# Quarter sums of weights: 29 of 128 additions moved from VectorE into accumulating transfers, in an encoder block on one core

## The chip, the cores and the metric

The kernel runs on one core of a Trainium2 chip. The metric is the device time of one execution in microseconds (us). The engines that matter here are TensorE (PE in the profile, PEld for its weight loads), VectorE (DVE), ScalarE (ACT), GpSimd (POOL), which also issues the DMAs that add while they write, and SyncE (SP), which issues the plain loads.

## The reference

One layer of an encoder on 512 tokens of width 1024, all in float32:

```
h    = RMSNorm(x);  proj = h @ W_in                      # 1024 x 11264
y_a  = (B * dwconv3(C * x_c)) @ W_a                      # 1024 x 1024
y_r  = (GroupNorm(Ret_fwd + Ret_bwd) * silu(G)) @ W_r    # 2048 x 1024, 4 heads
x    = x + (sigmoid(gA) * y_a + sigmoid(gR) * y_r) @ W_o # 1024 x 1024
h2   = RMSNorm(x)
x    = x + (silu(h2 @ W_gate) * (h2 @ W_up)) @ W_down    # 1024 x 2816, 2816 x 1024
y    = RMSNorm(x)
```

The result has to keep float32 accuracy.

## The kernel before, in words

**Split products.** Every float32 operand is split in two numbers that TensorE takes at full rate: `split` (L200) lets ACT round the source into `hi` (a CAST at L203), and VectorE subtracts, `lo = source - hi` (L204). A product is then three matmuls: hi hi, hi lo and lo hi.

**Seven products instead of eight.** Most weight matrices are used as quads: two by two quarters b11, b12, b21, b22. Strassen's scheme in Winograd's form multiplies seven combinations instead of eight quarters. On the weight side the seven forms are b11, b21, b22 and four sums (`FORMS`, L55):

```
t1 = b11 + b12      t2 = b11 + b12 + b22      t4 = b11 + b12 + b22 + b21
t3 = b12 + b22
```

The sums are made in place, in the tiles into which the quarters were loaded: t1, t2 and t4 one after the other in b11's tile, t3 in b12's. `prefetch_form` (L290) does this with an addition on VectorE (L301), and then splits the tile into `whi` and `wlo`. The tiles come from three pools: ten `raw` buffers for quarters, five `whi` and five `wlo` for split units of 128 x 1024.

**The quads.** There are six of the input projection (kind `w`; the first of them, at column `C_V`, is the first head's), three of the convolution columns (`x`), W_a (`a`), W_o (`o`), eleven of gate and up (`f`, 0 to 10, called pairs below, since b11 and b21 belong to gate, b12 and b22 to up), and three of W_down (`d`, after pairs 2, 6 and 10; the number in the quad is its first pair). Kinds `w`, `a`, `o` and `d` take two units for each form (u = 0 and 2), the others one. For three quads, `SUMMED` (pairs 0 and 1, and W_o), the four sums are made in DRAM long before by copies and accumulating DMAs (`sum_step`, L265), and are loaded as they are. For the other quads the 128 additions at L301 are made: 48 for `w`, 12 for `x`, 8 for `a`, 36 for `f` and 24 for `d`.

**The order.** `plan()` (L71) lists all units in the order in which TensorE uses them. `take()` (L321) hands out the next unit and calls `prefetch()` (L306) until two further units (`AHEAD`) are split; `prefetch` first calls `load_raws` (L281), which issues the loads of quarters that the plan needs within four more places (`LEAD`). So a unit's load, addition, cast and subtraction stand in the source some two products ahead of its own matmuls. What each engine executes in which order is fixed when the program is built, from estimates of when each instruction can run; it can differ from the order in the source.

**A pair** (`pair`, L1173) takes, from pair 5 on, the forms t1, t2, b21, t3, b11 of the next pair, t4, b22; from pair 2 to 4 the forms t1, t2, t3, one b11 or b21 of a later pair, t4, b22. Pairs 2 to 4 have used their own b11 and b21 earlier (`FIRST_PRODUCTS`, `beside`). Each form is one product of 24 matmuls (L383). The products t2, t3 and t4 add onto one bank of PSUM; `snap` (L432, a copy by ACT at L434) reads it out between them: u2 after t2, u3 after t3. `gated` (L1125) makes the activations for `down`.

**Down** (`strassen`, L437, with `prod_tm`, L409) uses the seven forms with 12 matmuls (L427) for a full unit. The first `down` stores its parts in DRAM (`put_first`, L1210); `add_first` (L1213) then adds them to `ydr` by eight accumulating DMAs of 256 KB on POOL, placed behind a small GpSimd operation (`mark`, L1247) that reads a tile which `gated` made in pair 3. The second `down` adds to `ydr` at L1208. The last one is written out at L1302 and reads `ydr` by accumulating DMAs into SBUF (`snap_y`, L1264).

Of the kernel before, what the change touches and what calls it, by code (L numbers as in the profile page):

```python
# [15 lines left out]
ALU = mybir.AluOpType  # L16
# [13 lines left out]
C_XC, C_GB, C_GC, C_Q, C_K, C_V, C_G, C_GA, C_GR = (  # L30
    0, 1024, 2048, 3072, 4096, 5120, 7168, 9216, 10240)
# [113 lines left out]


SUMMED = (("f", 0), ("f", 1), ("o",))


def parts(quad):  # L150
    return (0, 2) if quad == ("o",) else (0,)


def loads():
# [3 lines left out]
    for i, x in enumerate(PLAN):  # L158
        if x[0] == "q":
            _, quad, name, u, nk = x  # L160
            need = name if quad in SUMMED else NEEDS.get(name)
            if need:
                out.append((i, quad, need, u, nk * WIDTH[quad[0]]))
    return out + [(len(PLAN), quad, "b12", u, QH) for quad in SUMMED for u in parts(quad)]

# [6 lines left out]
def block_kernel(ctx: ExitStack, tc: tile.TileContext, xw0, xw, xT, xtok, wpack, wquad, cols, decs, rot, g_ffn, g_final, out):  # L172
    nc = tc.nc
# [14 lines left out]
    def bigtile(dt=F32, n=4):  # L188
        return big.tile([P, n, 512], dt, tag="big", name="big", padded_shape=[P, 4, 512])
# [10 lines left out]
    def split(src, hi, lo, scale=None, round=None):  # L200

        if scale is None:
            first = (round or nc.scalar.copy)(hi, src)  # L203
            low_of[0] = nc.vector.tensor_tensor(out=lo, in0=src, in1=hi.bitcast(F32), op=ALU.subtract)  # L204
        else:
            first = nc.scalar.activation(hi, src, AF.Copy, scale=scale)
            nc.vector.scalar_tensor_tensor(
                out=lo, in0=src, scalar=scale, in1=hi.bitcast(F32),
                op0=ALU.mult, op1=ALU.subtract)
        return first  # L210
# [10 lines left out]
    pos = [0]  # L221
# [5 lines left out]
    def unit():  # L227
        hi = wpool.tile([P, QH], F32R, tag="whi", name="whi")
        lo = wpool.tile([P, QH], F32R, tag="wlo", name="wlo")
        return hi, lo  # L230

    def prefetch_block(loads, splits):
        i = block[0]
        block[0] += 1
        st = [rawtile(), rawtile()]
        units = []
        for c in range(2):
            if loads:
                loads(c)
            nc.sync.dma_start(st[c], wpack[i][:, c * QH:(c + 1) * QH])  # L240
        for c in range(2):
            hi, lo = unit()
            units.append((hi, lo))
            split(st[c], hi, lo)
            if splits:
                splits(c)
        return units

    raws = {}

    wsum = {(quad, f, u): dram.tile([P, QH], F32, name="_".join(map(str, (f, u, *quad))))
            for quad in SUMMED for u in parts(quad) for f in ("t1", "t2", "t3", "t4")}

    def quarter(quad, name, u):
        return wquad[next(i for i, x in enumerate(QUARTERS) if x[1:4] == (quad, name, u))]

    def sums_of(quads):
        return [(quad, f, g, u, add) for group in (
            (("t1", "b11", 0), ("t3", "b22", 0)), (("t1", "b12", 1), ("t3", "b12", 1)),
            (("t2", "t1", 0),), (("t2", "b22", 1),), (("t4", "t2", 0),), (("t4", "b21", 1),))  # L260
            for quad in quads for f, g, add in group for u in parts(quad)]

    steps = {"quads": sums_of(SUMMED[:2]), "heads": sums_of(SUMMED[2:])}

# [16 lines left out]
    def load_raws(upto):  # L281
        while loaded[0] < len(LOADS) and LOADS[loaded[0]][0] <= upto:
            _, quad, name, u, n = LOADS[loaded[0]]
            t = rawtile()
            src = wsum[quad, name, u] if name[0] == "t" else quarter(quad, name, u)
            nc.sync.dma_start(t[:, 0:n], src[:, 0:n])
            raws[quad, name, u] = t
            loaded[0] += 1

    def prefetch_form(quad, f, u, nk):  # L290


        n = nk * WIDTH[quad[0]]
        if quad in SUMMED:
            here, more = f, None
        else:
            here = {"t1": "b11", "t2": "b11", "t4": "b11", "t3": "b12"}.get(f, f)
            more = {"t1": "b12", "t2": "b22", "t4": "b21", "t3": "b22"}.get(f)
        t = raws[quad, here, u][:, 0:n]
        if more:  # L300
            nc.vector.tensor_tensor(out=t, in0=t, in1=raws[quad, more, u][:, 0:n], op=ALU.add)  # L301
        hi, lo = unit()
        split(t, hi[:, 0:n], lo[:, 0:n])
        return [(hi, lo)]

    def prefetch(first=False, loads=None, splits=None):  # L306
        i = pos[0]
        if i >= len(PLAN):
            return False
        pos[0] += 1  # L310
        x = PLAN[i]
        if not first:
            load_raws(i + LEAD)
        if x[0] == "c":
            units = prefetch_block(loads, splits)
        else:
            units = prefetch_form(*x[1:])
        ready.append((x, units))
        return True

    def take():  # L321
        if not ready:
            prefetch()
        x, units = ready.pop(0)
        while sum(len(u) for _, u in ready) < AHEAD and prefetch():
            pass
        return x, units
# [203 lines left out]
    def split_two(k):  # L531
        split_x(k)
        split_x(k + 1)
    prefetch(True, lambda c: load_x(4 + 2 * c), lambda c: split_two(4 + 2 * c))
    rcs = misctile(D, "rcs").rearrange("p (i n) -> p i n", i=2)
    nc.sync.dma_start(rcs, rot)
# [101 lines left out]
    for h in range(EARLY):  # L638
# [27 lines left out]
        t = bigtile()  # L666
# [281 lines left out]
    for h in range(HEADS):  # L948
# [5 lines left out]
        t = sg  # L954
# [469 lines left out]
```

## Time and profile before

| What | us |
|---|---|
| median of 3 runs (1023.52 to 1023.67) | 1023.57 |
| span of the profiled execution | 1021.7 |
| TensorE busy in that span | 1013.2 |
| VectorE busy | 902.5 |
| ScalarE busy | 548.4 |
| GpSimd busy | 151.7 |

The profiled execution is one of its own; its span runs from the first to the last instruction of the program. The other times in the text are read from its trace.

How to read the lines: a row of the groups gives line, engine, operation, the tile written and the tiles read, shapes and count; behind the bar the busy time of the group in us, the mean of one in ns, and the idle time of the engine just before them, with what ended it. A row of the chain or of a timeline starts with the time from the span's start and the duration. A row of the windows gives the stretch, its length, and for PE, PEld, DVE, ACT and POOL the busy us with the number of instructions, then the granted share of TensorE's clock, the busy share of the DMA engines and GB/s. A row of the DMA view ends with KB for each and the median time from issue to landing. TensorE's clock was granted in full over the span (mean 0.999).

### The profile page before, as it was taken

Reading aid. Unit: us, or ns where it says so; the run is one execution under the profiler, and the core shown is the slowest. Engines: PE = TensorE matmul, PEld = TensorE weight load, DVE = VectorE, ACT = ScalarE, POOL = GpSimd, SP = SyncE. Lnnn points to the kernel's source line nnn. Section 1 sums busy time; section 2 is a strip of 40 time slices with the busy share of each in tenths; the row PEclk is TensorE's granted clock in tenths of the full one; section 3 lists DMA queues with packets and bytes.
Section 4 is the critical chain, followed back from the end, with each engine's and each line's share of the span. In section 5 each row is a group of like instructions: output and inputs, shape, how many; then the busy total and the mean of one; then the engine's idle time right before and its main releaser. Section 6 shows DMA issues by size and latency. Waiting matters only on the chain.

```text
span 1021.7 us, 14821 instructions
## 1 busy us (share of the span) xinstructions
PE 1013.2 (99%) x5586; PEld 883.2 (86%) x5586; DVE 902.5 (88%) x1161; ACT 548.4 (54%) x744; POOL 151.7 (15%) x238
## 2 busy tenths in 40 slices
PE   9999999999999999999999999999999999999997
PEld 7888888888888998888888888889998999899986
DVE  7878998979798888797989997999898999889996
ACT  7547665553655455343543325586654565556554
POOL 0030221222122003202122100020001410110011
PEclk9999999999999999999999999999999999999999
DMA  9525587695767657839597855484316562663523
GB/s 354 188 81 185 173 296 212 214 310 162 249 196 238 250 203 268 333 130 349 124 331 294 272 200 169 157 264 132 107 42 242 172 154 83 198 153 104 165 69 98
DMA packets 53992, 202.34 MB, mean 198 GB/s; under 512 B 7392, under 2 KB 7520, under 8 KB 49312
## 3 DMA queue, kind: packets, MB, share of 16 engines
q1 hardware_dynamic: 37600, 137.39, 39.0%
q0 software_dynamic: 16032, 63.71, 21.3%
q8 instruction: 44, 0.72, 0.3%
q10 hardware_dynamic: 288, 0.29, 0.1%
q14 instruction: 28, 0.23, 0.1%
HBM read 162.82 MB, written 57.41 MB: 216 GB/s over the span
## 4 chain that ended last, share of the span: by engine, by line
PE 98%; DVE 1%; ACT 0%; issue 0%; POOL 0%; POOLq 0%; ACTq 0%
PE bank L427 39%; PE bank L383 27%; PE bank L342 10%; PE bank L343 10%; PE bank L344 10%; PE bank L477 0%; PE bank L1053 0%; PE bank L998 0%; PE bank L662 0%; DVE raw L301 0%; DVE big L1296 0%; ACT whi L203 0%; DVE wlo L204 0%; POOL fin L1286 0%; POOL ac L1035 0%
## 5 line engine op out<-in xcount | busy, mean ns | idle before, releaser
L203 ACT CAST whi<-raw 128x1024 fp32r<-128x1024 f32 (+2 forms) x299 | 302.8, 1028 | 265.0 <-PE bank L427 67.1
L204 DVE TENSOR_TENSOR wlo<-raw,whi 128x1024 fp32r<-128x1024 f32 (+2 forms) x300 | 352.7, 1192 | 68.0 <-ACT whi L203 67.7
L383 PE MATMUL bank<-xform,whi 128*128 128x256 f32 x1424 | 258.2, 284 | 0.3 <-ACT whi L203 0.3
L383 PEld LDWEIGHTS bank<-xform,whi 128*128 128x128 f32 x1424 | 222.3, 192 | 2.0 <-ACT t L434 0.8
L383 PE MATMUL bank<-xform,wlo 128*128 128x256 f32 x712 | 200.7, 283 | 0.0
L427 PE MATMUL bank<-whi,big 128*128 128x512 f32 x596 | 187.0, 389 | 0.0
L427 PE MATMUL bank<-whi,xform 128*128 128x512 f32 x496 | 157.1, 390 | 0.0
L301 DVE TENSOR_TENSOR raw<-raw 128x1024 f32<-128x1024 f32 (+1 forms) x128 | 152.0, 1203 | 4.2 <-DMA raw<-wquad 3.3
L383 PEld LDWEIGHTS bank<-xform,wlo 128*128 128x128 f32 x712 | 136.4, 192 | 0.0
L427 PEld LDWEIGHTS bank<-whi,big 128*128 128x128 f32 x596 | 111.9, 188 | 23.8 <-ACT t L434 0.4
L427 PE MATMUL bank<-wlo,big 128*128 128x512 f32 x298 | 115.7, 389 | 0.0
L427 PEld LDWEIGHTS bank<-whi,xform 128*128 128x128 f32 x496 | 93.0, 188 | 19.7 <-DVE xform L204 0.6
L427 PE MATMUL bank<-wlo,xform 128*128 128x512 f32 x248 | 96.5, 389 | 0.0
L434 ACT COPY t<-bank 128x512 f32<-128x512 f32 x105 | 61.0, 587 | 56.3 <-PE bank L383 30.1
L342 PE MATMUL bank<-big,whi 128*128 128x512 f32 x220 | 85.7, 390 | 0.0
L344 PE MATMUL bank<-big,wlo 128*128 128x512 f32 x220 | 85.6, 389 | 0.0
L343 PE MATMUL bank<-big,whi 128*128 128x512 f32 x220 | 85.6, 389 | 0.0
L427 PEld LDWEIGHTS bank<-wlo,big 128*128 128x128 f32 x298 | 56.0, 188 | 11.4
L427 PEld LDWEIGHTS bank<-wlo,xform 128*128 128x128 f32 x248 | 46.6, 188 | 9.6
L342 PE MATMUL bank<-whi,big 128*128 128x512 f32 x128 | 49.8, 389 | 0.0
L343 PE MATMUL bank<-wlo,big 128*128 128x512 f32 x128 | 49.8, 389 | 0.0
L344 PE MATMUL bank<-whi,big 128*128 128x512 f32 x128 | 49.8, 389 | 0.0
(203 smaller groups left out, 1385.8 us busy)
## 6 DMA issues: line engine op xcount, KB each, us to landing
raw<-wquad SPq DMA_DIRECT2D x140, 512.0 KB, 4.7
raw<-wpack SPq DMA_DIRECT2D x42, 512.0 KB, 6.3
t_f<-wquad POOLq DMA_DIRECT2D x12, 512.0 KB, 8.0
z<-t POOLq DMA_DIRECT2D x24, 256.0 KB, 4.5
t_o<-wquad POOLq DMA_DIRECT2D x12, 512.0 KB, 6.7
zform<-z POOLq DMA_DIRECT2D x6, 1024.0 KB, 7.8
v<-t POOLq DMA_DIRECT2D x16, 256.0 KB, 5.7
sg<-t POOLq DMA_DIRECT2D x16, 256.0 KB, 4.8
```

Source lines behind the costliest of these rows:

```text
L203: first = (round or nc.scalar.copy)(hi, src)
L204: low_of[0] = nc.vector.tensor_tensor(out=lo, in0=src, in1=hi.bitcast(F32), op=ALU.subtract)
L301: nc.vector.tensor_tensor(out=t, in0=t, in1=raws[quad, more, u][:, 0:n], op=ALU.add)
L342: nc.tensor.matmul(ps, lh, rh, start=first, stop=False)
L343: nc.tensor.matmul(ps, lh, rl, start=False, stop=False)
L344: nc.tensor.matmul(ps, ll, rh, start=False, stop=last)
L383: nc.tensor.matmul(o, l[:, c], r[:, k], start=start and s == 0 and k == 0 and i == 0, stop=stop and k == 3 and i == 2, skip_group_check=True)
L427: nc.tensor.matmul(pss[tt], l, r[:, c], start=start and k == 0 and i == 0, stop=stop and k == n - 1 and i == 2, skip_group_check=True)
L434: nc.scalar.copy(t, ps)
```

## The change

A predicate `joined(quad, name)` is new. It holds for t3 and t4 of W_a, of the three `down` quads and of the first head's quad, and for t4 alone of pairs 2 to 10. For these units L301 is left out. The addition is made by a DMA on POOL's queue instead, which reads the second quarter from DRAM and adds it to the tile in SBUF: b22 onto b12's tile once t1 has read it, b21 onto b11's tile once t2 was split. The DMA is put on a list when t1 or t2 is prefetched, and issued in the source at the end of the same call of `prefetch` for pairs, one call later for the others. The quarters b21 and b22 are loaded for their own products as before.

```
+def joined(quad, name):
+    kind = quad[0]
+    if quad in SUMMED or name not in ("t3", "t4"):
+        return False
+    return kind in "ad" or kind == "f" and name == "t4" or kind == "w" and quad[1] == C_V

 in prefetch_form:
-        if more:
+        if more and not joined(quad, f):
             nc.vector.tensor_tensor(out=t, in0=t, in1=raws[quad, more, u][:, 0:n], op=ALU.add)
         hi, lo = unit()
         split(t, hi[:, 0:n], lo[:, 0:n])
+        for g, after, src, add in (("t3", "t1", "b12", "b22"), ("t4", "t2", "b11", "b21")):
+            if f == after and joined(quad, g):
+                late.append((pos[0] + (quad[0] != "f"), raws[quad, src, u], quarter(quad, add, u), n))
         return [(hi, lo)]

+    late = []
+    def join_late():
+        while late and late[0][0] <= pos[0]:
+            _, t, src, n = late.pop(0)
+            nc.gpsimd.dma_start(out=t[:, 0:n], in_=src[:, 0:n], accum_op=ALU.add)

 at the end of prefetch:
         ready.append((x, units))
+        join_late()
         return True
```

## The prediction

> **What bounds the kernel now.** I read the page from the top: busy times, then the chain that ended last, then TensorE's own waits, and then the few microseconds in which TensorE was not working.
>
> ```profile
> span 1021.7 us, 14821 instructions
> PE 1013.2 (99%) x5586; PEld 883.2 (86%) x5586; DVE 902.5 (88%) x1161; ACT 548.4 (54%) x744; POOL 151.7 (15%) x238
> PE 98%; DVE 1%; ACT 0%; issue 0%; POOL 0%; POOLq 0%; ACTq 0%
> L301 DVE TENSOR_TENSOR raw<-raw 128x1024 f32<-128x1024 f32 (+1 forms) x128 | 152.0, 1203 | 4.2 <-DMA raw<-wquad 3.3
> ```
>
> TensorE is busy 1013.2 of 1021.7 us and carries 98% of the chain. VectorE is at 88%, but it matters only where TensorE waits for it. The additions at L301, which the change thins out, take 152.0 us of an engine that is not the limit. So the question is how much of TensorE's 8.5 idle us lies behind them. The view of waits, kept to TensorE, and the last of the 25 us windows answer it:
>
> ```profile
> PE bank L477 <- DVE t L474: 1.4, 1, 1.4
> PE bank L1053 <- DVE t L1039: 0.5, 1, 0.5
> PE bank L383 <- ACT whi L203: 0.3, 1, 0.3
> 1000.00:1025.00 25.00, 15.61 (x69) 12.58 (x68) 14.21 (x24) 9.65 (x22) 4.11 (x8) 0.93 0.22 85
> ```
>
> The first wait, 1.4 us, is the start of the program. The second, 0.5 us, is the norm ahead of the FFN. In the last window TensorE works 15.6 us, so it ends near 1015.6, and 6.1 us of final evictions and stores follow. The sum 1.4 + 0.5 + 0.3 + 6.1 is 8.3 of the 8.5 us. Only the 0.3 us has a weight split behind it, and the chain of waits shows what stood there:
>
> ```profile
> 756.88 24.86 PE bank L427 x108
> 781.74 0.84 DVE raw L301
> 782.58 0.28 issue
> 782.85 1.22 DVE wlo L204
> 784.07 2.28 DVE raw L301 x2
> 786.43 1.06 ACT whi L203
> 787.53 73.91 PE bank L383 x612
> ```
>
> This is the passage from the first `down` to pair 3. An addition on VectorE, a subtraction, two more additions, then ACT's cast, and TensorE goes on. It is the one place in the span where L301 ends a wait of TensorE.
>
> **What is removed.** `joined` holds for t3 and t4 of W_a (2 units each: 4), of the first head (4), of the three `down` quads (12), and for t4 of pairs 2 to 10 (9): 29 of the 128 additions. At the mean of 1.203 us that is 34.9 us of VectorE. Almost all of it lies beside matmuls that do not wait, and is worth nothing; the most it can give back is the 0.3 us above. Four of the 29 lie in that first `down`, two of them at full width, and for pairs 2 to 4 the b21 tile is no longer held until t4's addition, which frees a raw buffer earlier. Both bring pair 3's splits forward by more than 0.3 us, so I take the wait as gone. What is late next there is nothing that TensorE sees: it then runs straight on. **Gain 0.3 us.**
>
> **What is added.** 29 accumulating DMAs on the POOL queue, nearly all of 512 KB, about 14.7 MB. POOL must issue them in its order, and the cast and the subtraction of t3 or t4 now wait for a landing. The trace has no DMA that adds 512 KB into SBUF. Its neighbours are the plain loads, the adds of 256 KB into SBUF, and the adds of 512 KB from DRAM to DRAM at L272 (the last row, from the view of that line):
>
> ```profile
> raw<-wquad SPq DMA_DIRECT2D x140, 512.0 KB, 4.7
> big<-ydr POOLq DMA_DIRECT2D x4, 256.0 KB, 4.5
> L1268 POOL DMA_DIRECT2D big<-ydr x4 | 3.5, 954 | 90.2 <-ACT big L1267 90.2
> ```
>
> ```profile
> DMA to landing us min/median/max: 5.4/8.0/13.1
> ```
>
> Twice the bytes of `big<-ydr` cannot be quicker than it, so 4.5 us is the lower end. The upper end is 13.1, the longest at L272. I take 6.0, between the add into SBUF and the median of 8.0, and nearer the quickest at L272: the destination is SBUF, and in the pairs few of POOL's DMAs run at once. POOL's own work, 29 times 0.95 or 28 us, goes onto an engine at 15%. While a new DMA waits there for t1's or t2's reads, what is queued behind it waits too: the first head's stores, the load of `ga` beside W_a, and the stores of `down`. POOL's timeline shows them:
>
> ```profile
> 95.53 1.14 POOL L633 DMA_DIRECT2D v<-t  x2 [20.48 <-DVE t L448]
> 595.46 0.53 POOL L973 DMA_DIRECT2D big<-ga  x1 [13.07 <-DVE big L939]
> 773.64 1.20 POOL L1211 DMA_DIRECT2D first_part<-t  x2 [85.15 <-DVE t L448]
> ```
>
> POOL stood idle 20, 13 and 85 us before them, for VectorE's results; the reads that a new DMA waits for belong to units that come before those results. I cost this queueing at 0; held by one transfer's issue it would be 1 us of a store that TensorE does not wait for. SP's loads stay the same in number.
>
> Is there time for 6 us? In the pairs TensorE runs without a break from 787.53 to 861.44: 73.91 / 612 is 0.1208 us for a matmul, so 2.90 for a product of 24. Counting back over pairs 6 and 5 (seven products each), pair 5's products start at 820.9 (t1), 823.8 (t2), 826.7 (b21), 829.6 (t3), 832.5 (b11 of pair 6), 835.4 (t4) and 838.3 (b22). Pair 4 has six, from 803.5, its t4 at 815.1; pair 3's t4 starts at 797.7. There is one cast of a raw tile for each unit, in the plan's order on ACT, so counting names them. VectorE's and ACT's timelines around pairs 3 to 5:
>
> ```profile
> 787.51 3.50 DVE L204 TENSOR_TENSOR wlo<-raw,whi 128x1024 fp32r<-128x1024 f32 x3
> 799.88 2.36 DVE L204 TENSOR_TENSOR wlo<-raw,whi 128x1024 fp32r<-128x1024 f32 x2 [0.57 <-ACT whi L203]
> 818.53 1.23 DVE L204 TENSOR_TENSOR wlo<-raw,whi 128x1024 fp32r<-128x1024 f32 x1 [1.11 <-ACT whi L203]
> ```
>
> ```profile
> 817.45 1.05 ACT L203 CAST whi<-raw 128x1024 fp32r<-128x1024 f32 x1 [1.47 <-DVE raw L301]
> 819.41 1.03 ACT L203 CAST whi<-raw 128x1024 fp32r<-128x1024 f32 x1
> 820.70 1.99 ACT L203 CAST whi<-raw 128x1024 fp32r<-128x1024 f32 x2
> 823.97 1.05 ACT L203 CAST whi<-raw 128x1024 fp32r<-128x1024 f32 x1
> 826.84 1.05 ACT L203 CAST whi<-raw 128x1024 fp32r<-128x1024 f32 x1 [0.74 <-PE bank L383]
> 827.79 0.62 ACT L203 CAST big<-t 128x512 fp32r<-128x512 f32 x1
> 828.32 0.58 ACT L434 COPY t<-bank 128x512 f32<-128x512 f32 x1
> ```
>
> The first row starts with pair 3's t2, the second with pair 4's, the third is pair 5's. The DMA may start when that subtraction ends: 788.7, 801.1 and 819.8. Until t4's product that leaves 9.0, 14.0 and 15.6 us. A cast (1.05) and a subtraction (1.22) must still follow, so the transfer has 6.7, 11.7 and 13.3 us. At 6.0 all three fit; at 8.0 pair 3 is late by 1.3 us, unless its splits come earlier, as above; at 13.1 it is late by 6.4 and pair 4 by 1.4. In the `down` quads and the two others six units lie between t2 and t4; at 24.86 / 108 = 0.230 us a matmul and twelve in a full unit that is 16.6 us, or 14.3 for the transfer.
>
> ACT's order is the second cover. On ACT stand, behind pair 5's t4 cast (823.97), b22's cast (826.84) and the copy of the bank at 828.32, which is u2: t3's product adds onto that bank and cannot start before the copy ends. In the source that copy stands ahead of both casts, so the queue's order is made when the program is built, by estimated readiness, and a DMA that is later than estimated holds the copy too. With a landing at 819.8 + 6.0 = 825.8, ACT is 1.8 us later at t4's cast, but b22's cast can start at 826.9, as before: nothing is lost. I cost the added wait at **0**; without that cover it costs what rival 1 says.
>
> Sum against the profiled execution: 1021.7 - 0.3 = 1021.4. The median of the runs shown is 1.87 us above its span; with that, **1023.3 us**.
>
> **Rivals.** Rival 1, slower: pair 5's DMA queues behind the eight adds of `add_first`. POOL's timeline, the landings of those eight, and VectorE beside POOL:
>
> ```profile
> 787.24 1.14 POOL L1211 DMA_DIRECT2D first_part<-t  x2 [4.05 <-DVE t L464]
> 805.94 7.34 POOL L1247 TENSOR_SCALAR mark<-t 128x1 f32<-128x1 f32 x1 [17.56 <-DVE t L1139]
> 813.24 6.82 POOL L1208 DMA_DIRECT2D ydr<-first_part  x8
> ```
>
> ```profile
> DMA to landing us min/median/max: 4.8/8.4/10.3
> ```
>
> ```profile
> 811.98 1.22 DVE L301 TENSOR_TENSOR raw<-raw 128x1024 f32<-128x1024 f32 x1
> 813.20 0.69 DVE L1192 TENSOR_TENSOR t<-bank,t 128x512 f32<-128x512 f32 x1
> ```
>
> POOL is taken until 820.06, and the last of the eight, issued at 818.4, lands some 10.3 us later, at 828.7. Behind it pair 5's transfer lands about 831, since POOL's DMAs share one queue. If t4's cast stays ahead of the copy of u2, then cast, b22's cast, the gate's cast and the copy end at 831 + 1.05 + 1.05 + 0.62 + 0.58 = 834.3 instead of 829.6, and TensorE stands for 4.7 us: 1023.3 + 4.7 = **1028.0**. It decides from a landing after 829.6 - 3.3 = 826.3. For it: VectorE is busy 69.73 of 74 us over pairs 3 to 6 (row below), so T0 does not move far. Against it: `mark` takes 7.34 us for a column of one, and ends just where VectorE's run of operations with two SBUF inputs ends (813.20, the first one that reads a bank). With 1.2 us less in each pair VectorE will pause sooner, the eight start earlier and the queue clears before 826; and the builder may put the copy first.
>
> ```profile
> 787.50:861.50 74.00, 73.97 (x613) 73.78 (x614) 69.73 (x85) 44.79 (x60) 14.96 (x11) 1.00 0.55 150
> ```
>
> Rival 2: transfers of 8 us, the median at L272, from sharing DMA engines that are 0.55 busy there. Pair 3 is late by 1.3 us, the others hold: 1023.3 + 0.3 + 1.3 = **1024.9**, still no change by the measure.
>
> Rival 3: POOL's issue itself is held by VectorE. Then each transfer starts up to 7.3 us later, as `mark` did. By ACT's order, pair 5's copy ends at 819.8 + 7.3 + 6.0 + 3.3 = 836.4, 6.8 us late; over the four pairs from 3 to 6 that is 27 us: **1050**. Against it: two issues at 787.24 took 1.14 us together, while the three subtractions from 787.51 ran.
>
> The Trainium skill, SBUF — State Buffer, section SBUF: two separate sides, says that a DMA issued from GpSimd starves while VectorE holds the shared ports; by that, rival 3. The same section limits the lock of operations with two SBUF inputs to GpSimd operations that read SBUF, and the trace agrees with this: `mark` waited 7.34 us, the two issues did not.
>
> Rival 4, faster: TensorE would have to win 2.05 us, but its waits other than start and end sum to 0.8 us.
>
> **How the numbers follow.** A measurement of this kernel can tell about 0.2%, 2.05 us, from no change. Forecast (1022.7 to 1024.0) 0.74; rival 2 (to 1025.6) 0.08; rival 1 (1025.6 to 1029) 0.13, since it needs both a late queue and that order; rival 3 0.03; rival 4 0.02. So faster 0.02, same 0.82, slower 0.16. The range from 1022.6, where all waits inside the span are gone and a little beside, to 1025.6 holds the first two, 0.82; it takes in transfers from 4.5 to 8 us, and those near 13.1 are rival 1's.
>
> **What would show it.** Right: 99 additions at L301; TensorE busy 1013 us still; no wait of TensorE for a cast near 786; the new DMAs landing in 4.5 to 8 us; ACT waiting for DMAs into raw tiles, without TensorE behind it. Wrong: a wait of TensorE for ACT's copy at L434 or a cast at L203 in the pairs, above all in pair 5 (rival 1), or POOL issues of several us (rival 3). What I would have misjudged then is the landing time, or the order that the builder gives ACT.

## The result, and the profile after

The changed kernel took 1037.47 us (median of 4 runs, 1035.9 to 1042.76) against 1023.55 us for the kernel before: a ratio of 1.0145, 95% interval 1.0118 to 1.0171. It is 14 us slower, where 1023.3 us and no change were predicted. The profiled execution took 1038.37 us and its span is 14.9 us longer than that of before. Its page, the busy times and the chain that ended last, and the group of the additions:

```profile
span 1036.6 us, 14890 instructions
PE 1018.2 (98%) x5586; PEld 886.8 (86%) x5586; DVE 874.1 (84%) x1132; ACT 548.3 (53%) x744; POOL 170.2 (16%) x267
PE 84%; issue 10%; DMA 2%; POOL 1%; DVE 1%; ACT 1%; POOLq 0%; ACTq 0%
L309 DVE TENSOR_TENSOR raw<-raw 128x1024 f32<-128x1024 f32 (+1 forms) x99 | 118.4, 1210 | 5.5 <-DMA raw<-wquad 4.6
```

(The change moves the lines: L301 is now L309, the cast L203 is L211, the product L383 is L403, the copy L434 is L454, `mark` is L1267.) The change does what it says: 99 additions are left, and VectorE works 28 us less. But TensorE's share of the chain falls from 98% to 84%. In its place stand transfers (2%) and 10% of what the profile calls issue, time in which it shows nothing that the engine waited for; most of that is the chain following POOL's queue back, so these shares are not the loss. TensorE's waits name the place:

```profile
PE bank L403 <- ACT t L454: 10.2, 5, 4.9
PE bank L497 <- DVE t L494: 1.4, 1, 1.4
PE bank L1073 <- DVE t L1059: 0.5, 1, 0.5
```

The 0.3 us for ACT's cast has gone, as predicted. New are five waits of a pair's product for the copy of a bank (L454), 10.2 us together. The distance between the starts of two matmuls beside each wait, less the usual 0.12 us, gives the whole stall:

| Pair | stall begins | us | its transfer: issue to landing |
|---|---|---|---|
| 2 | 745.3 | 0.85 | 6.3 |
| 3 | 792.8 | 2.35 | 7.0 |
| 5 | 834.1 | 5.07 | 11.2 |
| 7 | 919.6 | 1.71 | 11.2 |
| 10 | 981.9 | 1.00 | 5.5 |
| sum | | 11.0 | |

Pairs 4, 6, 8 and 9 have no stall; their transfers took 5.4 to 5.5 us. What ACT does in pair 3 (first two rows) and pair 5 (the others), from its timeline:

```profile
793.64 1.04 ACT L211 CAST whi<-raw 128x1024 fp32r<-128x1024 f32 x1 [6.59 <-DMA raw<-wquad]
794.59 0.58 ACT L454 COPY t<-bank 128x512 f32<-128x512 f32 x1
...
834.57 1.04 ACT L211 CAST whi<-raw 128x1024 fp32r<-128x1024 f32 x1 [7.48 <-DMA raw<-wquad]
835.52 1.13 ACT L211 CAST big<-t 128x512 fp32r<-128x512 f32 x2
836.56 1.04 ACT L211 CAST whi<-raw 128x1024 fp32r<-128x1024 f32 x1
838.16 0.62 ACT L211 CAST big<-t 128x512 fp32r<-128x512 f32 x1 [0.57 <-DVE t L1175]
838.69 0.58 ACT L454 COPY t<-bank 128x512 f32<-128x512 f32 x1
```

Read it from below. The copy (u2) is what t3's product waits for. It needs nothing from the new DMA, but ACT works in its order, and ahead of the copy stands the cast of t4, which now waits for the landing: ACT sits idle 6.59 and 7.48 us. TensorE's timeline in pair 3 shows the other end, the last matmul of t1's product and the first of t3's:

```profile
792.75 0.28 PE L403 MATMUL bank<-xform,wlo 128*128 128x256 f32 x1
795.22 0.38 PE L403 MATMUL bank<-xform,whi 128*128 128x256 f32 x1 [2.19 <-ACT t L454]
```

Pair 5's transfer lands late behind what was issued ahead of it on POOL's queue (experiment 5 moves that away). POOL's timeline, and the landings of the eight adds of `add_first`:

```profile
811.24 0.33 POOL L1267 TENSOR_SCALAR mark<-t 128x1 f32<-128x1 f32 x1 [7.38 <-DVE t L1159]
811.53 6.82 POOL L1228 DMA_DIRECT2D ydr<-first_part  x8
823.27 0.91 POOL L323 DMA_DIRECT2D raw<-wquad  x1 [4.92 <-DVE wlo L212]
...
906.46 1.78 POOL L1228 DMA_DIRECT2D ydr<-t  x2 [3.39 <-ACT t L454]
907.57 1.57 POOL L323 DMA_DIRECT2D raw<-wquad  x1
```

```profile
DMA to landing us min/median/max: 4.9/11.3/14.0
```

The eighth add was issued at 816.7 and landed 14.0 us later, at 830.7; pair 5's transfer, issued at 823.27, landed at 834.5. Pair 7's was issued at 907.57, right behind two adds of the second `down` (the last two rows). Over the 27 transfers of 512 KB the median is what was estimated (from the view of DMAs):

```profile
raw<-wquad POOLq DMA_DIRECT2D x27, 512.0 KB, 6.1
```

The stalls are 11.0 of 14.9 us. The rest is the clock. Windows of pair 3 (first two rows), of pair 5 (the next three) and of pair 7, columns as in the windows before:

```profile
792.50:795.00 2.50, 0.53 (x5) 0.32 (x3) 0.29 (x1) 1.36 (x2) 0.00 (x0) 1.00 1.00 397
795.00:800.00 5.00, 4.78 (x27) 4.78 (x28) 4.53 (x4) 2.17 (x4) 0.00 (x0) 0.66 0.60 183
834.00:839.30 5.30, 0.41 (x4) 0.20 (x2) 3.14 (x6) 4.17 (x7) 0.00 (x0) 0.76 0.01 2
839.30:842.00 2.70, 2.68 (x12) 2.68 (x13) 2.70 (x4) 0.91 (x1) 0.00 (x0) 0.50 0.54 170
842.00:845.00 3.00, 3.00 (x21) 3.00 (x20) 1.87 (x2) 0.57 (x1) 0.00 (x0) 0.73 0.57 197
915.00:925.00 10.00, 8.45 (x71) 8.25 (x70) 6.14 (x6) 3.84 (x5) 0.00 (x0) 1.00 0.85 222
```

After pair 3's stall the granted share is 0.66 over 5 us. With the clock at half speed for a part of it (the row from 839.30 shows 0.50), that part is 0.34 x 5.0 / 0.5 = 3.4 us, and 1.7 us of work are lost. Around the end of pair 5's stall the three rows give (0.24 x 5.3 + 0.50 x 2.7 + 0.27 x 3.0) / 0.5 = 6.9 us at half speed; 4.3 of them (2.7 + 1.6) lie behind the stall and lose 2.15 us. Behind pair 7's stall of 1.71 us the clock stays at 1.00. Sum: 11.0 + 1.7 + 2.15 = 14.85 us, as good as the 14.9 us between the spans (the 0.3 us gained is not in the sum). That is the profiled execution; over the four runs the mean granted clock goes from 0.996 (1035.9 us) to 0.992 (1042.76 us), so the clock's part differs from run to run.

### The profile page after: what moved, and what is told of

Same layout as the page of the kernel before. It is cut to its first block, busy times and chain, and to the rows that moved or that the text cites. A ratio compares the mean times of both kernels' runs of the same rounds, so it can differ in the third digit from the quotient of the medians.

```text
span 1036.6 us, 14890 instructions
## 1 busy us (share of the span) xinstructions
PE 1018.2 (98%) x5586; PEld 886.8 (86%) x5586; DVE 874.1 (84%) x1132; ACT 548.3 (53%) x744; POOL 170.2 (16%) x267
## 4 chain that ended last, share of the span: by engine, by line
PE 84%; issue 10%; DMA 2%; POOL 1%; DVE 1%; ACT 1%; POOLq 0%; ACTq 0%
PE bank L447 36%; PE bank L403 17%; PE bank L362 10%; PE bank L363 10%; PE bank L364 10%; DMA raw<-wquad 2%; POOL ydr L1228 1%; PE bank L497 0%; PE bank L682 0%; PE bank L1018 0%; POOL first_part L1231 0%; ACT t L454 0%; ACT whi L211 0%; DVE big L1316 0%; POOL raw L323 0%
## 5 line engine op out<-in xcount | busy, mean ns | idle before, releaser
L211 ACT CAST whi<-raw 128x1024 fp32r<-128x1024 f32 (+2 forms) x299 | 303.8, 1028 | 283.1 <-PE bank L447 68.4
L403 PE MATMUL bank<-xform,whi 128*128 128x256 f32 x1424 | 261.6, 286 | 10.2 <-ACT t L454 10.2
L403 PEld LDWEIGHTS bank<-xform,whi 128*128 128x128 f32 x1424 | 224.9, 194 | 12.5 <-ACT t L454 11.8
L403 PE MATMUL bank<-xform,wlo 128*128 128x256 f32 x712 | 202.5, 285 | 0.0
L447 PE MATMUL bank<-whi,big 128*128 128x512 f32 x596 | 187.9, 390 | 0.0
L403 PEld LDWEIGHTS bank<-xform,wlo 128*128 128x128 f32 x712 | 138.1, 194 | 0.0
L309 DVE TENSOR_TENSOR raw<-raw 128x1024 f32<-128x1024 f32 (+1 forms) x99 | 118.4, 1210 | 5.5 <-DMA raw<-wquad 4.6
L454 ACT COPY t<-bank 128x512 f32<-128x512 f32 x105 | 61.1, 585 | 59.7 <-PE bank L403 30.5
L323 POOL DMA_DIRECT2D raw<-wquad x29 | 26.7, 922 | 252.7 <-DVE wlo L212 179.7
L362 PE MATMUL bank<-whi,big 128*128 128x512 f32 x128 | 49.8, 389 | 0.0
```

The lines of the kernel that those rows point to most:

```text
L323: nc.gpsimd.dma_start(out=t[:, 0:n], in_=src[:, 0:n], accum_op=ALU.add)
L362: nc.tensor.matmul(ps, lh, rh, start=first, stop=False)
L403: nc.tensor.matmul(o, l[:, c], r[:, k], start=start and s == 0 and k == 0 and i == 0, stop=stop and k == 3 and i == 2, skip_group_check=True)
L447: nc.tensor.matmul(pss[tt], l, r[:, c], start=start and k == 0 and i == 0, stop=stop and k == n - 1 and i == 2, skip_group_check=True)
L454: nc.scalar.copy(t, ps)
```

## The experiments

**Theory A:** the price lies in the pairs and in ACT's order. t4's cast waits for its transfer with the copy of u2 behind it; a queue on POOL lengthens some of these waits. **Rival B:** the 14.7 MB of new traffic slows the loads or the other transfers. A second question is what VectorE's relief is worth.

**1. Which of the joins.** First all but the pairs, then the pairs alone:

```
     joined, e1_no_pairs:
-    return kind in "ad" or kind == "f" and name == "t4" or kind == "w" and quad[1] == C_V
+    return kind in "ad" or kind == "w" and quad[1] == C_V
     joined, e2_pairs_alone:
+    return kind == "f" and name == "t4"
```

> The 9 additions of pairs 2 to 10 go back to VectorE; the 20 of W_a, down and the first head stay with the DMAs. Theory A (ACT's cast of a pair's t4 waits for the landing with the copy of u2 behind it): nothing of that is left, about 1023.2 us, TensorE busy about 1013. Theory B (14.7 MB more traffic and longer DMA queues make weights late): 20 of 29 transfers stay, so about two thirds of the 14 us, 1032 to 1034.

> Only the 9 additions of pairs 2 to 10 are made by DMAs. Theory A: the whole loss, 1034 to 1041 us, with TensorE waiting for ACT's copy in several pairs. Theory B: about a third of it, near 1028.

Without the pairs: 1023.05 us, ratio 0.9997 (0.9987 to 1.0006). With the pairs alone: 1038.87 us, 1.0146 (1.0128 to 1.0165). TensorE's waits, first without the pairs, then with the pairs alone:

```profile
PE bank L497 <- DVE t L494: 1.4, 1, 1.4
PE bank L1073 <- DVE t L1059: 0.5, 1, 0.5
```

```profile
PE bank L403 <- ACT t L454: 10.2, 5, 5.0
PE bank L447 <- ACT big L211: 1.6, 2, 1.1
```

The whole loss is in the nine joins of the pairs. Which of them stall depends on the build: with the pairs alone pair 4 stalls (2.1 us, at 810.2), and pairs 2 and 3 do not (less than 0.3 us). The other twenty, which have six units between t2 and t4, cost nothing, and gain nothing that a measurement can tell.

**2. What the relief is worth.** The 29 transfers are left out with the additions:

```
             if f == after and joined(quad, g):
-                late.append((pos[0] + (quad[0] != "f"), raws[quad, src, u], quarter(quad, add, u), n))
+                pass
```

> The 29 additions are left out, neither VectorE nor a DMA makes them, so those t3 and t4 lack their last quarter. It shows what the relief of VectorE alone is worth. Both theories: 1023.2 us, the 0.3 us before pair 3 gone and nothing else. If it is slower than 1025, the new instruction order itself costs time and both theories miss a part.

1022.92 us, 0.9994 (0.9985 to 1.0003). So even additions that cost nothing anywhere would not have made the kernel measurably faster.

**3. The traffic without the wait.** The nine transfers of the pairs are issued at the same place in POOL's order and after the same subtraction, but add into a tile in DRAM that nobody reads; VectorE makes the pairs' additions.

```
-        if more and not joined(quad, f):
+        if more and not (quad[0] != "f" and joined(quad, f)):
...
-                late.append((pos[0] + (quad[0] != "f"), raws[quad, src, u], quarter(quad, add, u), n))
+                late.append((pos[0] + (quad[0] != "f"), unread if quad[0] == "f" else raws[quad, src, u],
+                             quarter(quad, add, u), n, low_of[0] if quad[0] == "f" else None))
...
+                add = nc.gpsimd.dma_start(out=t, in_=src, accum_op=ALU.add, max_dma_last_dim=4 * CH)
+                tc.add_manual_dep(add.ins, low.ins.name, mybir.DependencyInfo(
...
```

> The nine transfers of the pairs are issued at the same points of POOL's queue, each after its t2 subtraction, but they add to a DRAM tile that nobody reads, and VectorE makes the pairs' additions as before; the other 20 stay as in the changed kernel. Theory A: no cast waits for them, 1023 to 1025 us. Theory B (traffic and queues): most of the 14 us stays, 1033 or more.

1022.97 us, 0.9998 (0.9989 to 1.0007). The view of DMAs shows the traffic was there (one of the ten sets the tile up):

```profile
unread<-wquad POOLq DMA_DIRECT2D x10, 512.0 KB, 5.5
```

Rival B falls: the transfers cost nothing; what costs is that something waits for them. (These nine land in DRAM, not in SBUF; experiment 6 has eight of them in SBUF, at no cost either.)

**4. The order on ACT.** All 29 joins stay, but t4's splits are ordered behind the copy of u2:

```
     snap:
-        nc.scalar.copy(t, ps)
+        copied[0] = nc.scalar.copy(t, ps)
     pair, both branches:
             u2 = snap(a)
+            u2_of[q] = copied[0]
     prefetch_form:
-        split(t, hi[:, 0:n], lo[:, 0:n])
+        if quad[0] == "f" and joined(quad, f):
+            with tc.issue_after(u2_of[quad[1]].ins):
+                split(t, hi[:, 0:n], lo[:, 0:n])
+        else:
+            split(t, hi[:, 0:n], lo[:, 0:n])
```

> All 29 as in the changed kernel, but the split of a pair's t4 is queued on ACT behind the copy of u2. Theory A: the copies no longer wait for a landing; 1023 to 1025 us, at most pair 5, whose transfer took 11.2 us, is late at t4 itself by a microsecond or two. Theory B: the traffic is the same, about 1037.

1027.47 us, 1.004 (1.0025 to 1.0055): 10 of the 14 us are back, fewer than expected. ACT's timeline in pair 5 and the landing of that pair's transfer (issued at 819.5):

```profile
826.56 0.58 ACT L458 COPY t<-bank 128x512 f32<-128x512 f32 x1
832.72 1.05 ACT L211 CAST whi<-raw 128x1024 fp32r<-128x1024 f32 x1 [5.58 <-DMA raw<-wquad]
```

```profile
DMA to landing us min/median/max: 13.1/13.1/13.1
```

The first row is u2's copy, now ahead of the cast. Four of the five stalls are gone. What is left are 2.2 us in pair 5, at 834.4, where the next copy (u3) stands behind the late cast, half speed after it (a granted share of 0.83 over 832 to 842), and 1.3 us at 867, where the first product of the second `down` waits for the casts of pair 6's gates.

**5. The queue on POOL.** `add_first` is placed three pairs later, behind an operation of pair 6 instead of pair 3 (`q_add = 6`): on the changed kernel, on experiment 4's, and on the kernel before.

```
-    q_add, gate_of = FF_PARTS[1][0], [None]
+    q_add, gate_of = 6, [None]
```

> The changed kernel with only those eight adds placed behind pair 6, the order on ACT as the builder makes it. Theory A with the queue as the cause of the 11.2 us: the stall of 5.1 us in pair 5 shrinks to 1 to 2 us and most of its 2 us of slow clock goes, 1031 to 1033 us; the stalls of the other pairs stay. If the queue is not the cause, 1037.

> As the run with the copy of u2 first (1027.5 us), and the eight adds of the first down's parts are placed behind pair 6 instead of pair 3. If what is left there, 2.2 us ahead of pair 5's t4 product and the slower clock after it, comes from pair 5's transfer standing behind those eight (13.1 us to landing), it lands in 5 to 7 us and the time falls to 1023.5 to 1025. If it comes from the traffic or from ACT being late in general, it stays near 1027.

> The kernel before with the eight adds placed behind pair 6, as a control for the two above. Nothing waits for them there: 1023.6 us, within 1 us.

On the kernel before it changes nothing: 1023.41 us, 1.0002 (0.9992 to 1.0011). On the changed kernel: ratio 1.0158 (1.0141 to 1.0175) from three runs of 1038.46 to 1041.32; a fourth took 1690.6 us at a mean granted clock of 0.556 and is left out of the ratio. With the copy first: 1034.16 us, 1.01 (1.0083 to 1.0117). Both expectations are missed, though the step they rest on holds: pair 5's transfer lands in 6.0 us in both, and its stall is gone. The queue found another victim. POOL's timeline and the landings of the two transfers at 875 and 878, with the copy first:

```profile
868.29 6.81 POOL L1234 DMA_DIRECT2D ydr<-first_part  x8
875.02 1.00 POOL L327 DMA_DIRECT2D raw<-wquad  x1
877.74 0.86 POOL L327 DMA_DIRECT2D raw<-wquad  x1 [1.71 <-DMA ydr<-first_part]
```

```profile
DMA to landing us min/median/max: 16.3/16.4/16.5
```

They are t4's two units of the second `down`. ACT's timeline there, and TensorE's wait:

```profile
891.57 1.04 ACT L211 CAST whi<-raw 128x1024 fp32r<-128x1024 f32 x1 [13.27 <-DMA raw<-wquad]
894.13 2.94 ACT L211 CAST whi<-raw 128x1024 fp32r<-128x1024 f32 x3 [1.51 <-DMA raw<-wquad]
896.98 1.06 ACT L458 COPY t<-bank 128x512 f32<-128x512 f32 x2
```

```profile
PE bank L451 <- ACT t L458: 9.0, 1, 9.0
```

It is the same form again: copies of banks that TensorE needs stand behind casts that wait for a landing. On the changed kernel this wait is 4.1 us. I had looked only at what the adds would leave, not at what they would meet. A transfer behind those eight takes long whichever it is (11.2 and 13.1 us in pair 5, 16.0 to 16.5 us here), and this also breaks the cover in a `down` quad, that is, the time that a transfer has before something waits for it.

**6. Order or queue alone.** First experiment 4's kernel without pair 5's join, then the changed kernel, its order untouched, without the joins of pairs 5 and 7, whose transfers took 11 us:

```
     e9_copy_first_not_5 (on e3_copy_first):
+    return kind in "ad" or kind == "f" and name == "t4" and quad[1] != 5 or kind == "w" and quad[1] == C_V
     e10_not_5_not_7 (on the changed kernel):
+    return kind in "ad" or kind == "f" and name == "t4" and quad[1] not in (5, 7) or kind == "w" and quad[1] == C_V
```

> The kernel with the copy of u2 ordered ahead of t4's splits, and pair 5's t4 summed on VectorE again; 28 of the 29 joins stay. Theory A (ScalarE's order sets the price, the queue on POOL lengthens it): with the order mended only pair 5 had a transfer too late for it, so its 2.2 us, the half-clock stretch of about 1.7 us behind it and the 1.3 us ahead of the second down's first product should go: 1022.5 to 1024, no wait of TensorE for ScalarE's copy, clock 0.999. Rival (the forced order itself costs): the time stays near 1027 without pair 5.

> The changed kernel without an edit of the order, but with pairs 5 and 7, whose transfers land in 11 us, summed on VectorE; 27 joins stay. If late landings alone were the cause (only the queue on POOL matters): about 1023.5, no stalls. Theory A (the order on ScalarE matters for every pair, even at landings of 5.5 to 7 us): the stalls of pairs 2, 3 and 10 stay, some 0.9 + 2.4 + 1.0 us, with 1.7 us of half clock behind the one of 2.4: 1027 to 1030.

The first: 1023.02 us, 0.9998 (0.9989 to 1.0007), with 28 of the 29 joins in place and no wait of a pair left. So the forced order costs nothing by itself. Pair 7's transfer, again behind two adds of the second `down`, took 11.8 us there, and TensorE does not wait for it. The second: 1031.62 us, 1.0078 (1.006 to 1.0095), above its expected 1027 to 1030 (its four runs go from 1029.0 us at a mean granted clock of 0.999 to 1033.23 us at 0.995, and the longest is the profiled one). TensorE's waits, of the first and of the second:

```profile
PE bank L501 <- DVE t L498: 1.4, 1, 1.4
PE bank L1077 <- DVE t L1063: 0.5, 1, 0.5
```

```profile
PE bank L403 <- ACT t L454: 4.8, 3, 3.2
PE bank L447 <- ACT big L211: 0.8, 1, 0.8
```

The stalls of pairs 2, 3 and 10 stay where no transfer is queued behind the eight. Pair 3's is 3.4 us here instead of 2.35, since its transfer is issued 1.0 us later; the clock answers with a granted share of 0.68 over 10 us, that is 6.4 us at half speed in this window:

```profile
796.00:806.00 10.00, 9.80 (x59) 9.80 (x60) 7.14 (x8) 4.62 (x6) 0.89 (x1) 0.68 0.43 130
```

So ACT's order alone, at landings of 5 to 7 us, costs about half of the loss (ratio 1.0078 against 1.0145), the late landings of pairs 5 and 7 the rest. With the order mended and pair 5's late transfer out of the way the other 28 joins are free. Theory A holds. A version faster than the kernel before did not come out of it; experiment 2 says why these 29 additions have none to give.

## Why the prediction was wrong

- **What bounds the kernel: right.** TensorE, and one wait of 0.3 us behind an addition. The wait is gone from the profile after, and its gain can't be measured (the ratios of experiment 1 without the pairs, of experiment 2 and of experiment 6's first run all have 1 in their intervals).
- **What is removed and added: right in number, and nearly in size.** 29 additions; VectorE's busy time fell by 28.4 us, where 34.9 were summed, but TensorE sees none of it; a median of 6.1 us for the transfers, where 6.0 was taken; POOL's issue 0.92 us (26.7 us for 29), where 0.95 was. The twenty joins with six units of cover cost nothing.
- **The step that failed: "I cost the added wait at 0".** The cover of pairs 3, 4 and 5 was counted to t4's own product ("at 6.0 all three fit"). But t4's cast stands ahead of u2's copy on ACT, so the deadline is the next thing behind the cast, and that is t3's product. The prediction saw this order and tried it for pair 5 only. The same sum from its own numbers, for pair 3: t4's product was counted to start at 797.7, two products behind t3's, so t3's was due at 797.7 - 2 x 2.90 = 791.9; the transfer could start at 788.7, and cast and copy take 1.05 + 0.58. That leaves 1.6 us, not 6.7. No transfer in the range of 4.5 to 13.1 us fits. Measured: 7.0 us to landing, and a stall of 2.35 us. It was still no certainty, because the order in pair 3 is new. In the kernel before, counting the casts as the prediction does, ACT has u2's copy ahead of t4's cast in pair 3 (the first of the three casts below); in pair 2 and in pairs 4 to 10 the cast was ahead already.

```profile
791.91 0.59 ACT L434 COPY t<-bank 128x512 f32<-128x512 f32 x1 [2.53 <-PE bank L383]
792.39 2.94 ACT L203 CAST whi<-raw 128x1024 fp32r<-128x1024 f32 x3
```

- **Rival 1: the right mechanism with too narrow a place.** It gave pair 5 4.7 us; the stall was 5.07. It was given 0.13, "since it needs both a late queue and that order". Experiment 6 shows that the order needs no late queue (pairs 2, 3, 10), and pair 7 has a late queue of its own, behind `down`'s adds.
- **The argument against rival 1: right in size, wrong in its reason and its end.** `mark` shrank from 7.34 to 0.33 us, but not because VectorE paused sooner. It came later, at 811.24, since the stalls of pairs 2 and 3 and the slow clock stood ahead of its input, and it fell into the 0.42 us of an operation with one input, just ahead of seven us of operations with two. VectorE's timeline after:

```profile
811.06 0.42 DVE L1175 TENSOR_TENSOR t<-t 128x256 f32<-128x256 f32 x1
811.40 0.76 DVE L1175 TENSOR_TENSOR t<-t,t 128x256 f32<-128x256 f32 x2
812.07 0.69 DVE L212 TENSOR_TENSOR big<-t,big 128x512 fp32r<-128x512 f32 x1
```

  The Trainium skill, SBUF — State Buffer, section SBUF: two separate sides, ties a wait like that of 7.34 us to VectorE's operations with two SBUF inputs; these rows agree. And the eight adds, issued 1.7 us earlier than before (811.53 against 813.24), still landed as late as 830.7. The burst had not cleared by 826.
- **A term that was missing: the clock.** 3.85 of the 14.85 us are matmuls at half speed behind two stalls. The sum took a stall at its own length.
- **Rivals 2 and 3: out.** Without a burst ahead, the pairs' transfers took 5.4 to 7.0 us, not 8; the longest of the 29 issues on POOL was 1.57 us, not 7. Rival 4 (faster) was rightly low.

Not settled: why the build's estimates place the cast ahead of the copy, and why they now do so in pair 3; only the effect of that order was tried.

## What to carry to other kernels

When an instruction is given a new wait, count its cover to the deadline of whatever stands behind it on its in-order engine, not to the deadline of its own result, and do it at every place of the same form. A DMA that someone waits for needs a look at what is ahead of it on its queue: moving the burst ahead of it only helps if nothing urgent stands behind its new place. And where an engine that is not the bound is relieved, leave the work out once: that run gives the most that any version could win.

## What was not expected of the hardware

- **Stalls of 2.2 us and more cost more than their length.** Behind 2.35 us TensorE's clock was at half speed for 3.4 us, around the end of 5.07 us for 6.9 us, and in experiment 5 with the copy first, around the end of the stall of 9.2 us, for some 10.3 (granted shares 0.63 and 0.87 below: (0.37 x 9.5 + 0.13 x 12.5) / 0.5). A stall of 2.1 us in the run with the pairs alone left it at 1.00 (third row below); 2.2 us in experiment 4 did not (0.83).

```profile
888.00:897.50 9.50, 0.56 (x3) 0.14 (x1) 3.51 (x4) 4.41 (x6) 0.10 (x1) 0.63 0.69 164
897.50:910.00 12.50, 12.39 (x48) 10.11 (x49) 9.68 (x11) 5.50 (x8) 6.10 (x7) 0.87 1.02 229
```

```profile
806.00:816.00 10.00, 8.06 (x67) 7.86 (x67) 8.00 (x14) 5.79 (x9) 6.07 (x9) 1.00 0.62 132
```

Where a stall lies seems to matter too. The two stretches at half speed in the changed kernel's profile begin at 795.83 and 836.79, 12 x 3.41 us apart; with the pairs alone they begin at 835.47 and 920.80, 25 x 3.41 us apart (read from windows of 0.1 to 0.3 us). Counted back by that step, the stall of 2.1 us (810.2 to 812.4) is split by a border at 811.6. This is an estimate from these stalls, and no run tests it.

The Trainium skill, TensorE: Matmul & The Clock Gate, section Part 1: The HAM clock gate (the "warmup" mystery), says that a free-running window of 3413 ns decides and that an idle window of about 3.4 us halves the clock. The stretches agree, being near one, two and three such windows. The idle time does not: 2.2 us were enough here, and the measurement decides.

- **A burst ahead of a transfer on POOL's queue holds it up for long.** In the changed kernel's pairs a transfer of 512 KB took 5.4 to 7.0 us where the queue ahead of it had drained. It took 11.2 to 16.5 us behind the eight adds of 256 KB, pair 5's with the first of them issued 12 us earlier, and 11.2 us behind two adds of the second `down` (pair 7). Whether it is the queue or the DMA engines that hold it up is not separated: the DMA engines' busy share is 1.10 in that stretch (row below), and the four plain loads that SP issued from 814 to 826 took 7.7 to 9.7 us, against 3.4 to 6.8 us for those from 740 to 811.

```profile
820.00:825.00 5.00, 5.00 (x44) 5.00 (x43) 3.89 (x4) 4.62 (x6) 0.91 (x1) 1.00 1.10 274
```
